# One-hot rows laid out by pairs of tokens, a reordered copy out of PSUM, and eleven low halves moved from DMA to VectorE, in a hybrid encoder layer

## The chip, the cores and the metric

The kernel runs on one core of one Trainium2 chip. The metric is the device time of one execution in microseconds (us). TensorE is PE in the profile (PEld is its weight load), VectorE is DVE, ScalarE is ACT, GpSimd is POOL, and SyncE, which issues most DMAs, is SP.

## What is computed

One encoder layer over 512 tokens of width 1024: a mixer (a gated linear recurrence beside chunked attention), cross-attention into 256 memory tokens, and an expert layer with 16384 single-neuron experts. Only the expert layer matters here. For each token, 8 heads select 16 experts each by product keys, so that a token has 128 selected experts with weights `g`:

```python
    def block(args):
        xt, it, gt = args
        u = expert_u[it]
        act = jax.nn.gelu(jnp.einsum('td,tkd->tk', xt, u))
        return jnp.einsum('tk,tkd->td', gt * act, expert_v[it])
```

An expert's number is `128 * i + j`, with `i` and `j` from the two key tables of its head.

## The kernel before

The first 128 tokens (tile 0) are done by gathering the rows of their experts. The other 384 tokens (tiles 1 to 3) are done densely: each of 128 blocks of 128 experts is multiplied with all 384 tokens, the result goes through the gelu and is multiplied by a dense weight that is zero where a token did not select the expert, and the second table then turns this into the output. Two things are therefore needed ahead of the dense second part, and the kernel makes them in the same stretch of its program.

**The dense weights.** For a token, the 128x128 matrix of weights is a product over its 128 selections: `hot` holds one-hot rows (column n of selection s is 1 where the expert's index equals n), `wei` holds the one-hot row of the other index times the weight, in two parts (a half-precision weight and its remainder). A group is four tokens. VectorE makes `hot` with one comparison (line 997) and `wei` with one product (line 1000), both 1024 half-precision elements per partition. PE then does eight matmuls (line 1003), two parts for each of four tokens, each with its own 128x128 weight load from `hot` and 128 columns of `wei`. ScalarE copies the result out of PSUM (line 1005) to a tile `stage`, which holds 16 tokens; when it is full, an SP DMA writes it to DRAM as `Wd` (line 1015, 1 MB). There are 96 groups and 24 such writes. The `hot` and `wei` tiles have three buffers each (`WGB`), `stage` has two. In the layout before, the token is the innermost index of `hot` and `wei`, with four tokens side by side: a matmul for one token reads every fourth element.

**The first multiplications, ahead.** Between the groups, PE multiplies expert blocks of the first table `U` with the 384 tokens (`mm1_parts`): 24 matmuls of 384 columns for each block, from a high half `wh` and a low half `wl` of the block (lines 111 to 113). ScalarE makes `wh` by a cast (line 131). The low half is `w - wh`, and it is made in one of two ways, which `source` decides by its third result: by DMA, where ScalarE writes `-w` rounded (line 137) and a POOL DMA then adds `w` to it (line 138); or by VectorE with one subtraction (line 149, in `fill_low`). `w`, `wh` and `wl` have three buffers each. Blocks 0 to 36 go by DMA, 37 and up by VectorE. Ten blocks are multiplied while VectorE prepares tile 1's selection; blocks 10 to 36 are spread over the 96 groups; then come blocks 37 to 39, and after these the second table's part, in which PE alternates between one block of `U` and one of `V`.

VectorE also does the selection of the next tile between the groups (`second_level`, lines 885 to 967). The order of instructions on each engine in this stretch comes from a scheduler that works at build time, from the program's order and priorities; from block 37 on the order is as written.

Of the kernel before, what the change touches and what calls it, by code (L numbers as in the profile page):

```python
# [12 lines left out]
F16 = mybir.dt.float16  # L13
# [3 lines left out]
AF = mybir.ActivationFunctionType  # L17
# [13 lines left out]
NE = 128  # L31
LAG = 40
# [4 lines left out]
NQ = 3  # L37
NORM_AT = (0, 6), (1, 2)
U_DMA = 3
U_V = ()  # L40
BY_DMA = ("pq",)
G_RATE = 2.45
G_END = 4
# [11 lines left out]
GS = float(2 ** 15)  # L55
# [20 lines left out]
def layer(ctx, tc, a, out, upto=99, dbg=None):  # L76
    nc = tc.nc
    dbg = dbg or {}
    V, A, PE, SP, PL = nc.vector, nc.scalar, nc.tensor, nc.sync, nc.gpsimd

    def pool(stack, name, bufs=1, **kw):
        return stack.enter_context(tc.tile_pool(name=name, bufs=bufs, **kw))
# [9 lines left out]
    def bank(name="bk"):  # L92
        return psum.tile([128, 512], F32, name=name, tag="bk")
# [65 lines left out]
    def source(kind, n):  # L159
# [5 lines left out]
        if kind == "U":  # L165
            return a["U"][n], [128, D], n < LAG - U_DMA and n not in U_V
        if kind == "V":
# [20 lines left out]
    def proj(key, ops, n=S, **kw):  # L188
        wh, wl = W.get(*key, **kw)
        ps = bank()  # L190
        mm3(ps[:, :n], [(wh[:, c], wl[:, c], h[:, :n], l[:, :n]) for c, (h, l) in enumerate(ops)])
        return ps
# [427 lines left out]
    for n in range(NCH):  # L620
        if n == 0:
            pair = close_pair(pair, [yo[c] for c in range(NCH)])
        ps = pair[n] if n < 2 else proj(("wo", n), [yo[c] for c in range(NCH)])
# [132 lines left out]
    with tc.tile_pool(name="hx", bufs=2) as hx:  # L756
        ho = []
        for c in range(NCH):
            t = hx.tile([128, S], F32, name="ht")
# [36 lines left out]
    def mm1_next():  # L796
        ahead[0] += 1
        return mm1_parts(ahead[0] - 1)

    top_pool = ExitStack()  # L800
    tp = pool(top_pool, "top")
    val = tp.tile([128, 8, 2, TT, 16], F32)
    idx = tp.tile([128, 8, 2, TT, 16], U32)

    io4 = tp.tile([128, NE, 4], F16)
    mio = tp.tile([128, 16, 8], F16)
    jr = tp.tile([128, 128], I32)
    PL.iota(jr, pattern=[[1, 128]], base=0, channel_multiplier=0)
    V.tensor_copy(io4, jr[:, :, None].to_broadcast([128, NE, 4]))
    V.tensor_copy(mio, jr[:, :16, None].to_broadcast([128, 16, 8]))  # L810


# [157 lines left out]
    def hurried(steps, offset):  # L970
        while True:
            with tc.high_priority(offset=offset) if offset else ExitStack():
                if next(steps, 0) == 0:
                    return
            yield

    with tc.tile_pool(name="wg", bufs=2) as wg, tc.tile_pool(name="st", bufs=2, side="right") as stages:
        parts, owed = iter(()), 0.0
        done = 0
        for k, _ in enumerate(hurried(second_level(1), OFF1)):  # L980
            while ahead[0] < LAG and done < (k + 1) * U_MID / 15 and done < U_MID:
                done += 1
                for _ in mm1_next():
                    pass
        rate = (LAG - SPARE - ahead[0]) * NCH / (DT * 32)
        for tile_ in range(1, TT):
            level = hurried(second_level((tile_ + 1) % TT), OFF2)
            ij, gg = SEL.pop(tile_)
            for q in range(8):
                tb = (tile_ - 1) * 8 + q  # L990
                stage = stages.tile([128, NE, 16], F32, name="stage", tag="stage")
                for t4 in range(0, 16, 4):
                    ps = bank()
                    gr = (q * 16 + t4) // 4
                    F4 = [128, 2, NE, 4]
                    hot = wg.tile(F4, F16, name="hot", bufs=WGB)
                    V.tensor_tensor(hot, io4[:, None].to_broadcast(F4), ij[:, gr, :, None].to_broadcast(F4),
                                    op=OP.is_equal)
                    wei = wg.tile(F4, F16, name="wei", bufs=WGB)
                    V.tensor_mul(wei, hot[:, 0:1].to_broadcast(F4), gg[:, gr, :, None].to_broadcast(F4))  # L1000
                    for k in range(4):
                        for part in range(2):
                            PE.matmul(ps[:, k * 128:(k + 1) * 128], hot[:, 1, :, k], wei[:, part, :, k],  # L1003
                                      start=part == 0, stop=part == 1)
                    A.activation(stage[:, :, t4:t4 + 4].rearrange("p i t -> p t i"),  # L1005
                                 ps.rearrange("p (t i) -> p t i", t=4), AF.Copy, scale=1.0 / GS)
                    if (q * 4 + t4 // 4) % LEVEL[1] < LEVEL[0]:
                        next(level, 0)
                    owed += rate
                    while owed >= 1:  # L1010
                        owed -= 1
                        if next(parts, 0) == 0 and ahead[0] < LAG - SPARE:
                            parts = mm1_next()
                            next(parts)
                SP.dma_start(Wd[:, tb], stage)
            for _ in level:
                pass
        for _ in parts:
            pass
        while ahead[0] < LAG - SPARE:  # L1020
            for _ in mm1_next():
                pass
        W.fill(W.used + 3)
# [227 lines left out]
```

## Time and profile before

| what | value |
| --- | --- |
| time, median of 3 runs | 1673.76 us (1672.78 to 1677.97) |
| the profiled execution's own time | 1675.25 us |
| its span, first to last instruction | 1673.5 us |
| busy share of the span: PE / DVE / ACT / POOL | 98% / 76% / 48% / 29% |
| first group of eight to the last, by the trace | about 549 to 757 us |
| mean granted TensorE clock | 0.996 |

Busy shares are means over a span whose stages have different limits. A busy PE is not a PE at its peak: a matmul's record lasts longer than the distance to the next matmul, so spacing is read from starts. A spacing times a count is PE's time; a mean length is not.

### The profile page before, as it was taken

How to read it: one execution, taken by the hardware profiler on the slowest of the kernel's cores; microseconds unless marked ns; L12 is line 12 of the kernel's file. 1: busy time of each engine (PE TensorE's matmuls, PEld its weight loads, DVE VectorE, ACT ScalarE, POOL GpSimd, SP SyncE). 2: the span in 40 equal slices, each digit the busy share in tenths (PEclk: the TensorE clock that was granted, in tenths of full speed). 3: DMA queues.
4: the chain of work that ended last, by engine and by line, in shares of the span. 5: the costliest groups of instructions: out<-in, count | busy, mean ns of one | idle time of the engine just before them, and what ended most of it. 6: DMA issues, size and time to landing. Idle time of an engine off the chain costs nothing.

```text
span 1673.5 us, 23775 instructions
## 1 busy us (share of the span) xinstructions
PE 1645.1 (98%) x8512; PEld 1443.6 (86%) x8512; DVE 1276.9 (76%) x2571; ACT 810.0 (48%) x1233; POOL 478.0 (29%) x346
## 2 busy tenths in 40 slices
PE   8999999999999999999999999999999999999997
PEld 6778888887779999999999999999999999988886
DVE  6778885555999888765777777777777777788887
ACT  5568753446446778873333333333333333333334
POOL 0010000001111111104544444445444445454331
PEclk9999999999999999999999999999999999999999
DMA  6345352127677898889988898898988988989994
GB/s 240 115 128 153 114 172 93 59 89 198 148 176 179 231 276 252 267 256 327 310 310 302 296 322 298 295 310 312 306 300 296 327 296 300 312 315 336 320 329 149
DMA packets 156934, 410.54 MB, mean 245 GB/s; under 512 B 13856, under 2 KB 62112, under 8 KB 153744
## 3 DMA queue, kind: packets, MB, share of 16 engines
q1 hardware_dynamic: 110016, 242.36, 42.5%
q0 software_dynamic: 46800, 166.68, 33.2%
q8 instruction: 66, 1.08, 0.3%
q14 instruction: 52, 0.43, 0.1%
HBM read 348.69 MB, written 29.36 MB: 226 GB/s over the span
## 4 chain that ended last, share of the span: by engine, by line
PE 88%; DVE 6%; DMA 2%; issue 2%; ACT 1%; SPq 0%; DVEq 0%; POOL 0%; POOLq 0%; ACTq 0%
PE acc L1106 31%; PE bk L111 15%; PE bk L113 15%; PE bk L112 15%; PE bk L1003 5%; DMA wl<-w 1%; PE pv L111 1%; PE pv L112 1%; PE pv L113 1%; DVE s L855 1%; DVE idx L853 1%; PE om L111 1%; PE om L112 1%; PE om L113 1%; DVE idx L859 1%
## 5 line engine op out<-in xcount | busy, mean ns | idle before, releaser
L131 ACT CAST wh<-w 128x1024 fp32r<-128x1024 f32 (+1 forms) x333 | 350.0, 1051 | 361.7 <-PE acc L1106 182.8
L111 PE MATMUL bk<-hH,wh 128*128 128x384 f32 (+1 forms) x1128 | 394.1, 349 | 0.0
L113 PE MATMUL bk<-hH,wl 128*128 128x384 f32 (+1 forms) x1128 | 386.1, 342 | 2.9 <-DMA wl<-w 2.7
L112 PE MATMUL bk<-hL,wh 128*128 128x384 f32 (+1 forms) x1128 | 385.3, 342 | 0.0
L149 DVE TENSOR_TENSOR wl<-w,wh 128x1024 fp32r<-128x1024 f32 (+1 forms) x280 | 340.2, 1215 | 27.8 <-ACT wh L131 27.1
L1036 POOL DMA_INDIRECT g<-in_Un,gidx x128 | 208.0, 1625 | 221.4 <-DVE junk L1043 210.7
L1036 POOL DMA_INDIRECT g<-in_V,gidx x128 | 202.1, 1579 | 240.0 <-DVE gacc L1053 225.1
L1106 PE MATMUL acc<-wh,ph 128*128 128x512 f32 x768 | 238.6, 391 | 0.0
L1106 PE MATMUL acc<-wh,pl 128*128 128x512 f32 x768 | 238.2, 391 | 0.0
L1106 PE MATMUL acc<-wl,ph 128*128 128x512 f32 x768 | 238.0, 390 | 0.0
L1083 DVE TENSOR_TENSOR pl<-act,ph 128x384 fp32r<-128x384 f32 x128 | 71.2, 557 | 199.9 <-ACT ph L1080 199.8
L111 PEld LDWEIGHTS bk<-hH,wh 128*128 128x128 f32 x1128 | 214.5, 190 | 7.3
L113 PEld LDWEIGHTS bk<-hH,wl 128*128 128x128 f32 x1128 | 212.4, 188 | 9.0 <-DMA wl<-w 4.7
L112 PEld LDWEIGHTS bk<-hL,wh 128*128 128x128 f32 x1128 | 213.3, 189 | 7.1
L787 ACT ACTIVATE act<-bk 128x384 f32<-128x384 f32 x128 | 63.6, 497 | 276.4 <-PE bk L113 276.4
L138 POOL DMA_DIRECT2D wl<-w x53 | 45.5, 858 | 522.7 <-ACT wl L137 431.3
L1106 PEld LDWEIGHTS acc<-wl,ph 128*128 128x128 f32 x768 | 144.1, 188 | 31.6
L1106 PEld LDWEIGHTS acc<-wh,pl 128*128 128x128 f32 x768 | 144.1, 188 | 31.1
L1106 PEld LDWEIGHTS acc<-wh,ph 128*128 128x128 f32 x768 | 142.9, 188 | 24.3
L1053 DVE SCALAR_TENSOR_TENSOR gacc<-g,gu,gacc 128x1024 f32<-128x1024 f32 x127 | 162.5, 1279 | 0.6
L1043 DVE SCALAR_TENSOR_TENSOR junk<-g,htok 128x1024 bf16<-128x1024 f32 x128 | 156.0, 1219 | 0.8
L1005 ACT ACTIVATE stage<-bk 128x512 f32<-128x512 f32 x96 | 102.9, 1097 | 39.9 <-PE bk L1003 34.9
(312 smaller groups left out, 2334.4 us busy)
## 6 DMA issues: line engine op xcount, KB each, us to landing
w<-in_U SPq DMA_DIRECT2D x128, 512.0 KB, 5.4
w<-in_V SPq DMA_DIRECT2D x128, 512.0 KB, 5.6
wl<-w POOLq DMA_DIRECT2D x53, 512.0 KB, 5.5
Wd<-stage SPq DMA_DIRECT2D x24, 1024.0 KB, 6.3
wt<-Wd SPq DMA_DIRECT2D x90, 256.0 KB, 7.0
w<-in_w_pq SPq DMA_DIRECT2D x16, 512.0 KB, 3.7
w<-in_w_in SPq DMA_DIRECT2D x15, 512.0 KB, 3.8
x<-in_xT SPq DMA_DIRECT2D x16, 256.0 KB, 6.0
```

The costliest lines, as they stand in the source:

```text
L111: PE.matmul(ps, lh, rh, start=first and c == 0, stop=False)
L112: PE.matmul(ps, lh, rl, start=False, stop=False)
L113: PE.matmul(ps, ll, rh, start=False, stop=last and c == n - 1)
L131: A.copy(wh[:, cs], w[:, cs])
L149: V.tensor_sub(wl[:, cs], w[:, cs], wh[:, cs].bitcast(F32))
L1003: PE.matmul(ps[:, k * 128:(k + 1) * 128], hot[:, 1, :, k], wei[:, part, :, k], start=part == 0, stop=part == 1)
L1005: A.activation(stage[:, :, t4:t4 + 4].rearrange("p i t -> p t i"), ps.rearrange("p (t i) -> p t i", t=4), AF.Copy, scale=1.0 / GS)
L1036: PL.indirect_dma_start(out=g, out_offset=None, in_=a[table], in_offset=bass.IndirectOffsetOnAxis(ap=gidx[:, k:k + 1], axis=0))
L1043: V.scalar_tensor_tensor(junk, g, 1.0, htok, op0=OP.mult, op1=OP.mult, accum_out=gu[:, st:st + 1])
L1053: V.scalar_tensor_tensor(gacc, g, gu[:, k:k + 1], gacc, op0=OP.mult, op1=OP.add)
L1083: V.tensor_sub(PS[e][1], ACT.pop(e), PS[e][0].bitcast(F32))
L1106: PE.matmul(acc[t, hf], lhs[:, ts], rhs[:, hf * 512:(hf + 1) * 512], start=e == 0 and part == 0, stop=e == NE - 1 and part == 2)
```

## The change

Three edits. **Pairs:** `hot` and `wei` are laid out by pairs of tokens, with two tokens innermost in place of four, so a matmul for one token reads every second element of a contiguous piece; the comparison and the product run over the same 1024 elements, with the selected index and the weight now repeated in runs of two. **The copy:** ScalarE's copy walks in the order of `stage` (expert index outside, four tokens inside): it writes runs of four neighbouring elements to `stage` and reads PSUM with a step of 128 elements from one to the next; before, it read PSUM straight through and wrote every sixteenth element. **Low halves:** `U_V` names blocks 26 to 39, so that blocks 26 to 36, eleven of them, get their low half from VectorE in place of ScalarE and a POOL DMA (37 to 39 had it from VectorE before).

```diff
-U_V = ()
+U_V = range(26, LAG)
...
-    io4 = tp.tile([128, NE, 4], F16)
+    io2 = tp.tile([128, NE, 2], F16)
...
-                    F4 = [128, 2, NE, 4]
+
+                    pairs = lambda x: x[:, gr].rearrange("p s (q k) -> p (s q) k", k=2)
+                    F4 = [128, 4, NE, 2]
                     hot = wg.tile(F4, F16, name="hot", bufs=WGB)
-                    V.tensor_tensor(hot, io4[:, None].to_broadcast(F4), ij[:, gr, :, None].to_broadcast(F4),
+                    V.tensor_tensor(hot, io2[:, None].to_broadcast(F4), pairs(ij)[:, :, None].to_broadcast(F4),
                                     op=OP.is_equal)
                     wei = wg.tile(F4, F16, name="wei", bufs=WGB)
-                    V.tensor_mul(wei, hot[:, 0:1].to_broadcast(F4), gg[:, gr, :, None].to_broadcast(F4))
+                    W4 = [128, 2, 2, NE, 2]
+                    V.tensor_mul(wei.rearrange("p (s q) n k -> p s q n k", s=2),
+                                 hot[:, None, 0:2].to_broadcast(W4),
+                                 gg[:, gr].rearrange("p s (q k) -> p s q k", k=2)[:, :, :, None].to_broadcast(W4))
                     for k in range(4):
                         for part in range(2):
-                            PE.matmul(ps[:, k * 128:(k + 1) * 128], hot[:, 1, :, k], wei[:, part, :, k],
-                                      start=part == 0, stop=part == 1)
-                    A.activation(stage[:, :, t4:t4 + 4].rearrange("p i t -> p t i"),
-                                 ps.rearrange("p (t i) -> p t i", t=4), AF.Copy, scale=1.0 / GS)
+                            PE.matmul(ps[:, k * 128:(k + 1) * 128], hot[:, 2 + k // 2, :, k % 2],
+                                      wei[:, 2 * part + k // 2, :, k % 2], start=part == 0, stop=part == 1)
+                    A.activation(stage[:, :, t4:t4 + 4], ps.rearrange("p (t i) -> p i t", t=4), AF.Copy,
+                                 scale=1.0 / GS)
```

VectorE's queue in the second half of the stretch, from the last step of the selection's weights on (`hot` and `wei` are the groups' tiles, `eq`, `rc`, `kn` and `sel` belong to the selection, `wl` is a block's low half; the numbers are the builder's names of buffers). Before:

```order
L967 SCALAR_TENSOR_TENSOR gg_7054<-bk_7049,gg_7054 128x32x4
L997 TENSOR_TENSOR hot_7141<-io4_3894,ij_6183 128x1024
L936 TENSOR_TENSOR eq_7653<-eq_7653 128x1024
L1000 TENSOR_TENSOR wei_7143<-hot_7141,gg_6184 128x1024
L997 TENSOR_TENSOR hot_7161<-io4_3894,ij_6183 128x1024
L936 TENSOR_TENSOR eq_7653<-eq_7653 128x512
L1000 TENSOR_TENSOR wei_7163<-hot_7161,gg_6184 128x1024
L997 TENSOR_TENSOR hot_7186<-io4_3894,ij_6183 128x1024
```

The same place now (lines 997 and 1000 have become 999 and 1003):

```order
L967 SCALAR_TENSOR_TENSOR gg_7050<-bk_7045,gg_7050 128x32x4
L999 TENSOR_TENSOR hot_7109<-io2_3894,ij_6183 128x1024
L999 TENSOR_TENSOR hot_7136<-io2_3894,ij_6183 128x1024
L1003 TENSOR_TENSOR wei_7111<-hot_7109,gg_6184 128x1024
L1003 TENSOR_TENSOR wei_7138<-hot_7136,gg_6184 128x1024
L931 TENSOR_TENSOR eq_7643<-rc_7578,mio_3895 128x2048
L999 TENSOR_TENSOR hot_7156<-io2_3894,ij_6183 128x1024
L933 TENSOR_TENSOR eq_7643<-eq_7643,kn_7641 128x2048
L1003 TENSOR_TENSOR wei_7158<-hot_7156,gg_6184 128x1024
L999 TENSOR_TENSOR hot_7181<-io2_3894,ij_6183 128x1024
L149 TENSOR_TENSOR wl_7203<-w_7122,wh_7123 128x1024
L1003 TENSOR_TENSOR wei_7183<-hot_7181,gg_6184 128x1024
```

A subtraction (`L149`) now stands in the queue between a group's `hot` and its `wei`, about every three to four groups, eleven times; the selection's steps stand a few groups later. Each subtraction stands three to five groups ahead of its block's first matmul on PE, and behind the cast of its `wh`.

ScalarE's queue in the same half of the stretch (`act` is a block's gelu). Before:

```order
L1005 ACTIVATE stage_7089<-bk_7090 128x4x128
L131 CAST wh_7127<-w_7126 128x1024
L787 ACTIVATE act_7110<-bk_7031 128x384
L1005 ACTIVATE stage_7089<-bk_7112 128x4x128
L137 ACTIVATE wl_7130<-w_7126 128x1024
L1005 ACTIVATE stage_7089<-bk_7140 128x4x128
L1005 ACTIVATE stage_7089<-bk_7160 128x4x128
L1005 ACTIVATE stage_7184<-bk_7185 128x4x128
L131 CAST wh_7205<-w_7204 128x1024
```

And now (line 1005 has become 1010):

```order
L1010 ACTIVATE stage_7085<-bk_7135 128x128x4
L1010 ACTIVATE stage_7085<-bk_7155 128x128x4
L1010 ACTIVATE stage_7179<-bk_7180 128x128x4
L131 CAST wh_7200<-w_7199 128x1024
L787 ACTIVATE act_7197<-bk_7128 128x384
L1010 ACTIVATE stage_7179<-bk_7209 128x128x4
L1010 ACTIVATE stage_7179<-bk_7229 128x128x4
L1010 ACTIVATE stage_7179<-bk_7249 128x128x4
L131 CAST wh_7295<-w_7294 128x1024
```

The eleven `wl` steps of line 137 are gone from ScalarE's queue, and so are the eleven DMAs of line 138 behind them on POOL's (53 before, 42 now). The copy has the same 512 elements per partition in another order. PE's queue has the same instructions; one or two of a block's matmuls stand on the other side of a group here and there.

## Rows read from the trace of the kernel before

**Rows 1.** The page, parts 1 and 4: engines, and the last chain by line.

```profile
PE 1645.1 (98%) x8512; PEld 1443.6 (86%) x8512; DVE 1276.9 (76%) x2571; ACT 810.0 (48%) x1233; POOL 478.0 (29%) x346
...
PE acc L1106 31%; PE bk L111 15%; PE bk L113 15%; PE bk L112 15%; PE bk L1003 5%; DMA wl<-w 1%; PE pv L111 1%; PE pv L112 1%; PE pv L113 1%; DVE s L855 1%; DVE idx L853 1%; PE om L111 1%; PE om L112 1%; PE om L113 1%; DVE idx L859 1%
```

**Rows 2.** Windows: busy time per engine (instructions), granted clock, DMA share.

```profile
core 0: us, PE busy (x) PEld busy (x) DVE busy (x) ACT busy (x) POOL busy (x), PEclk, DMA share, GB/s
...
530.00:540.00 10.00, 7.97 (x44) 7.51 (x44) 10.00 (x76) 5.72 (x8) 1.44 (x3) 1.00 0.99 245
...
549.00:657.00 108.00, 107.80 (x740) 98.74 (x739) 93.93 (x266) 86.11 (x101) 12.28 (x15) 1.00 0.87 252
657.00:757.00 100.00, 100.00 (x688) 91.93 (x687) 71.56 (x118) 78.56 (x91) 9.43 (x11) 1.00 0.88 265
...
757.00:800.00 43.00, 43.00 (x231) 40.55 (x230) 26.63 (x38) 16.02 (x24) 21.11 (x14) 1.00 0.95 334
800.00:1600.00 800.00, 800.00 (x3981) 719.94 (x3979) 608.82 (x767) 281.26 (x388) 378.42 (x234) 1.00 0.90 309
```

**Rows 3.** Chain that ended last, 549 to 757 us: by line, one piece.

```profile
by line: PE bk L1003 43.5%; PE bk L111 18.4%; PE bk L113 18.4%; PE bk L112 18.2%; DMA wl<-w 3.0%; PE bk L959 0.3%; issue 0.0%
...
645.27 0.96 PE bk L1003 x8
```

**Rows 4.** Timeline of PE around a group of eight: start, length, instruction.

```profile
644.93 0.34 PE L113 MATMUL bk<-hH,wl 128*128 128x384 f32 x1
645.11 1.12 PE L1003 MATMUL bk<-wei,hot 128*128 128x128 f16 x8
645.98 0.43 PE L111 MATMUL bk<-hH,wh 128*128 128x384 f32 x1
646.25 0.34 PE L112 MATMUL bk<-hL,wh 128*128 128x384 f32 x1
```

**Rows 5.** PE matmuls by form, whole span: busy us, mean ns, idle before.

```profile
L1003 PE MATMUL bk<-wei,hot 128*128 128x128 f16 x768 | 107.4, 296 | 0.0
...
L522 PE MATMUL po<-ph,v 128*128 128x384 f32 x8 | 2.7, 337 | 0.0
...
L522 PE MATMUL po<-ph,v 128*128 128x256 f32 x8 | 2.2, 281 | 0.0
...
L522 PE MATMUL po<-ph,v 128*128 128x128 f32 x8 | 1.8, 223 | 0.0
```

**Rows 6.** VectorE groups by form, whole span.

```profile
L149 DVE TENSOR_TENSOR wl<-w,wh 128x1024 fp32r<-128x1024 f32 x278 | 338.8, 1219 | 25.8 <-ACT wh L131 25.0 <-PE bk L1003 0.6
...
L997 DVE TENSOR_TENSOR hot<-io,ij 128x1024 f16<-128x1024 f16 x96 | 66.2, 691 | 36.8 <-PE bk L1003 35.6
L1000 DVE TENSOR_TENSOR wei<-hot,gg 128x1024 f16<-128x1024 f16 x96 | 65.4, 686 | 0.8
```

**Rows 7.** ScalarE groups by form, whole span.

```profile
L1005 ACT ACTIVATE stage<-bk 128x512 f32<-128x512 f32 x96 | 102.9, 1097 | 39.9 <-PE bk L1003 34.9 <-DMA Wd<-stage 1.7 <-ACT kn L929 1.4
...
L137 ACT ACTIVATE wl<-w 128x1024 fp32r<-128x1024 f32 x53 | 56.8, 1071 | 0.0
...
L101 ACT CAST qh<-bk 128x512 fp32r<-128x512 f32 x13 | 7.5, 579 | 0.0
...
L929 ACT CAST kn<-idx 128x128 f16<-128x128 uint32 x8 | 6.4, 796 | 0.5 <-DVE eq L933 0.5
...
L101 ACT CAST k<-kr 128x128 fp32r<-128x128 f32 x16 | 4.8, 306 | 1.5 <-DMA kr<-in_keysT 1.5
```

**Rows 8.** DMA, 549 to 657 us: queues, issues of low halves.

```profile
q1 hardware_dynamic: 3680, 19.14, 48.3%
q0 software_dynamic: 2170, 7.91, 38.6%
...
wl<-w POOLq DMA_DIRECT2D x15, 512.0 KB, 5.6
```

More of the change, by code (lines that the diff above doesn't have):

```diff
@@ L808, in layer @@
     PL.iota(jr, pattern=[[1, 128]], base=0, channel_multiplier=0)
-    V.tensor_copy(io4, jr[:, :, None].to_broadcast([128, NE, 4]))
+    V.tensor_copy(io2, jr[:, :, None].to_broadcast([128, NE, 2]))
     V.tensor_copy(mio, jr[:, :16, None].to_broadcast([128, 16, 8]))
```

## The prediction, made before the changed kernel was run

> **What bounds the kernel now.** I read the page first: PE is busy 98% of the span, and the chain that ended last names the eight-matmul groups of line 1003 with 5% [rows 1]. A mean over stages says little about this change, so I then cut the trace into windows. Groups run from 549 to 757 us. There the reader is to see that PE is busy without a gap, that VectorE has 93.9 of 108 us and then 71.6 of 100, ScalarE 86.1 and 78.6, and that the DMA engines are busy 0.87 and 0.88 of the time [rows 2]. PE is the bound, and three others stand close behind it. The chain inside that stretch agrees: 43.5% of it is line 1003, 55% the 384-column matmuls of `U`, one wait for a low half's DMA stands at its start, and there is no VectorE or ScalarE in it [rows 3]. After the stretch PE is busy all of the time up to 1600 us [rows 2]: whatever the stretch gets shorter by, everything behind it moves forward by the same, because it is a fixed amount of PE work.
>
> What a group costs on PE is read from starts. The chain has 0.96 us for eight matmuls [rows 3], and the timeline gives the same: from 645.11 to 646.25 us are the eight and one L111 matmul, whose usual distance to the next is 0.18 (644.93 to 645.11), so the eight have 0.96 us, 120 ns each [rows 4]. Of the 208 us, 96 x 0.96 = 92 are the groups and 116 the `U` blocks.
>
> **Pairs, on PE.** Is 120 ns for 128 columns much? Line 522 has matmuls of 128, 256 and 384 columns that lie side by side: 223, 281 and 337 ns, so 128 columns cost 57 ns. The 128 columns of line 1003, of which neighbours lie four elements (8 bytes) apart, have 296 ns: 73 more than the 223 [rows 5]. That is what reading at about half the rate would give. The pairs put neighbours 4 bytes apart, which is also the distance of neighbours in line 522's 4-byte data, at the full rate. No row shows half-precision data read at that step, so the saving for a matmul lies between 0 and 73 ns. I take 49 (120 becomes about 71): nearer to line 522, as its bytes lie at the new distance, but under 57, since the weight load before each matmul must now hide behind less. That is 8 x 49 = 0.39 us a group, and 37 us of PE time over 96 groups, far more than will be gained, because the others stop it first.
>
> **Pairs, on VectorE.** `hot` and `wei` take 691 and 686 ns for 1024 elements, while the subtraction of 1024 4-byte elements takes 1219 [rows 6]: half-precision runs of four go two at a time. No row has runs of two. Bounds: 691 and 686 as now, or up to 1219 each. I take no change, since a run of two still holds one whole pair. The smaller `io2` conversion, once, costs less than before and lies ahead of the groups.
>
> **The copy.** 512 elements out of PSUM in 1097 ns; the same count read and written straight takes 579 [rows 7]: the scattered write costs some 520 ns. Afterwards the write goes in runs of four and the read jumps. No row has a jumping read of PSUM. Bounds: 579, and upwards the dearest scattered access that ScalarE shows, 128 elements in 796 ns against 306 straight, 3.8 ns an element [rows 7], which would make 579 + 512 x 3.8 = 2.5 us. I take 0.6 to 1.1. Within that it costs nothing and gives nothing: ScalarE's other work is 86.1 - 50 x 1.10 = 31 us in the first window's 50 groups and 28 in the second's 46, so that with 1.1 us copies it stays at 86 and 79. Its cover ends near 1.3 us in the first window (31 + 50 x 1.3 = 96).
>
> **Low halves.** Eleven steps of 1071 ns leave ScalarE [rows 7] and eleven DMAs leave POOL's queue, which nothing behind them waits for before the stretch ends. On the DMA engines one such low half is dear: 38.6% of 108 us over 15 of them is 2.8 us each [rows 8]; eleven make 31 us, all of it for blocks 26 to 36, which is about the second window. VectorE gets 11 x 1219 ns = 13.4 us [rows 6], in the second window alone. The subtraction waits for the cast of `wh`; behind it in VectorE's queue stand the group's `wei` and all later groups, for which PE waits. Over its 278 present uses that wait is 25.0 us, 0.09 each [rows 6]; at worst each of the eleven waits for one whole cast, 11 x 1.07 = 12 us. I take 3, since it stands three to five groups ahead of its block and PE has up to two groups ready.
>
> **The sum.** First window (108 us): PE 107.8 - 50 x 0.39 = 88; VectorE 94; DMA 0.87 x 108 = 94. VectorE and DMA tie, and each can be filled: from 530 to 540 us VectorE was busy 10.00 of 10.00 and the DMA engines 0.99 [rows 2]. Together they will not reach this; I take 98, a gain of 10. Second window (100 us): PE 100 - 46 x 0.39 = 82; VectorE 71.6 + 13.4 = 85; DMA 88 - 31 = 57; ScalarE 67 or less. The bound is VectorE; with 3 us of waits, and one for its steps standing unevenly, 89, a gain of 11. Together 21 us: the span of 1673.5 becomes 1652.5, and the profiled execution's 1675.25 becomes 1654. The three runs' median is 1.5 us lower than that execution, less than what counts here; I predict 1654. This hardly depends on the 49 ns: any spacing under about 90 ns leaves PE below 96 and 89. A measurement of this kernel can tell about 0.3%, 5 us, from no change.
>
> **A. The step is not what the eight matmuls cost.** Then the spacing stays at 120 ns, for the weight load or the half-precision operand itself might set it. Against it is the 73 ns over line 522; for it, that those rows differ in data type as well. PE stays the bound in both windows, VectorE's 85 of 100 fits beneath it, and the DMA relief lies under it: 1674, 1671 to 1677. Chance 0.14. [...]
>
> **B. The reordered read of PSUM is dear** (ends slower). ScalarE needs 31 + 28 - 12 = 47 us besides the copies; with 96 copies of x us it fills the present 208 us at x = 1.67, and from there each further 0.1 us costs 10 us. At the upper bound of 2.5 us: 47 + 240 = 287, 79 more than 208: 1753; at 2.0 us: 1705. For it: scattered accesses are what is dear in every such row. Against: the dearest price is that of 2-byte writes, and the present scattered access of this same copy costs 1.0 ns an element, which as a read makes 1.1 us. Chance 0.09. [...]
>
> **C. VectorE loses its two at a time** (slower). Both products go to about 1219 ns, 1.06 us more a group: 94 + 53 = 147 and 85 + 49 = 134 us, 281 in place of 208: 1747. It decides from where the two together take (208 - 179) / 96 = 0.3 us more a group. Against it: runs of four already go at double rate with one operand that repeats. Chance 0.06.
>
> **D. The subtractions hold up VectorE's queue.** With the full 12 us of waits the second window is VectorE's 97, and the gain is the first window's 10 and 3 more: 1661. If the DMA engines give no more than 0.9 in the first window, as in the 800 us up to 1600 [rows 2], that window is 104 and the gain 4 + 11: 1659. Either is faster still; chance 0.12.
>
> **How the numbers follow.** The forecast, a gain of 15 to 29 us with 1654 as its likeliest, has 0.59; D 0.12, A 0.14, B 0.09, C 0.06. Faster: 0.59 + 0.12 = 0.71; within 0.3%: A, 0.14; slower: 0.15. The lowest time that the other engines allow is VectorE's alone, 94 + 85 = 179 of 208 us, 1646 with the own time's offset; four more for rows that a faster copy or quieter DMA engines shorten: 1642. Upwards the range takes in D and A: 1677. What it leaves out, B, C and a little below, is under 0.2.
>
> **What would show it.** Right: the L1003 matmuls near 223 ns in place of 296 and about 0.57 us for eight in the chain; idle time of PE before L1003's weight loads that waits for `wei` or `hot`, and no more idle time of `hot` that waits for PE; VectorE above 0.95 in both windows; `hot` and `wei` still near 690; the copy under 1.3 us; DMA share near 0.95 before block 26 and 0.65 after. The group stretch is then some 187 us long. Wrong: 296 ns again (A); a copy above 1.6 us with ScalarE busy throughout (B); `hot` over 0.8 us (C); VectorE idle before line 149 by over half a us each (D). It would also be wrong if the PE work behind the stretch started no earlier, because the last of `Wd` or of the `U` blocks came no earlier.

## The result, and the profile after

The changed kernel takes 1644.15 us (median of four runs, 1643.66 to 1645.27), the kernel before 1673.86 us beside it (1672.78 to 1677.97): a ratio of 0.9819 (95% interval 0.9802 to 0.9836), 30 us less. The profiled execution took 1643.93 us, its span is 1642.1 us. The forecast was 1654 with 1642 to 1677 as its range: right in direction and mechanism, with the gain put 10 us too small.

The page, parts 1 and 4, which answer to [rows 1]:

```profile
PE 1609.1 (98%) x8512; PEld 1407.3 (86%) x8512; DVE 1280.6 (78%) x2582; ACT 757.0 (46%) x1222; POOL 467.3 (28%) x335
...
PE acc L1111 31%; PE bk L111 15%; PE bk L113 15%; PE bk L112 15%; DMA wl<-w 2%; PE bk L1008 2%; PE pv L111 1%; PE pv L112 1%; PE pv L113 1%; DVE s L855 1%; DVE idx L853 1%; PE om L111 1%; PE om L112 1%; PE om L113 1%; DVE idx L859 1%
```

PE is busy 36 us less, with as many instructions, and the groups' line (1008, it was 1003) has fallen from 5% of the chain to 2%.

The 96 groups now start at 552.7 and end at 723.9 us, 171 us in place of 206. The windows of the first 50 groups, the other 46, and what lies behind them, as in [rows 2]:

```profile
core 0: us, PE busy (x) PEld busy (x) DVE busy (x) ACT busy (x) POOL busy (x), PEclk, DMA share, GB/s
552.70:643.50 90.80, 87.34 (x740) 77.77 (x739) 89.19 (x263) 63.11 (x99) 12.00 (x14) 1.00 0.99 290
643.50:723.90 80.40, 79.08 (x676) 70.81 (x675) 78.00 (x129) 47.99 (x80) 0.00 (x0) 1.00 0.72 257
724.00:800.00 76.00, 76.00 (x399) 70.80 (x398) 51.40 (x73) 27.03 (x38) 35.66 (x24) 1.00 0.93 323
800.00:1570.00 770.00, 770.00 (x3827) 692.49 (x3827) 586.08 (x734) 270.60 (x374) 363.33 (x226) 1.00 0.90 309
```

PE is no longer full in the first two windows. In the first, VectorE is busy 89.2 of 90.8 us and the DMA engines 0.99 of the time, both at once; in the second, VectorE 78.0 of 80.4, while the DMA engines have come down to 0.72. Behind the groups PE is full as before, so the gain is carried to the end: the last group comes 31.7 us earlier (755.6 to 723.9), the end of the span 31.4.

A group on PE, against [rows 4]:

```profile
564.14 0.34 PE L113 MATMUL bk<-hH,wl 128*128 128x384 f32 x1
564.32 0.64 PE L1008 MATMUL bk<-wei,hot 128*128 128x128 f16 x8
564.76 0.42 PE L111 MATMUL bk<-hH,wh 128*128 128x384 f32 x1
565.02 0.34 PE L112 MATMUL bk<-hL,wh 128*128 128x384 f32 x1
```

From 564.32 to 565.02 us are eight matmuls and one of L111; less the L111's usual 0.18 that leaves 0.52 us, and the chain below has 0.48, where it was 0.96. From one start to the next within a group are 58 ns (median over all 768; before 118 by the same reading).

The same operations as in [rows 5 to 7], by form:

```profile
L1008 PE MATMUL bk<-wei,hot 128*128 128x128 f16 x768 | 61.9, 221 | 2.8 <-DVE wei L1003 1.5 <-ACT stage L1010 1.0
...
L999 DVE TENSOR_TENSOR hot<-io,ij 128x1024 f16<-128x1024 f16 x96 | 64.3, 680 | 0.3 <-PE bk L1008 0.2
L1003 DVE TENSOR_TENSOR wei<-hot,gg 128x1024 f16<-128x1024 f16 x96 | 64.7, 684 | 0.0
...
L1010 ACT ACTIVATE stage<-bk 128x512 f32<-128x512 f32 x96 | 56.6, 610 | 56.5 <-PE bk L1008 29.2 <-DMA Wd<-stage 21.3 <-PE bk L112 3.5
```

The matmul went from 296 to 221 ns, `hot` and `wei` hardly moved (680 and 684), the copy went from 1097 to 610. `hot` used to wait 35.6 us for PE [rows 6]; now 0.2. A wait that has grown is the copy's, from 1.7 us [rows 7] to 21.3, for the write of `Wd` out of one of the two `stage` tiles.

The chain from 549 to 735 us, by line, and its pieces from 589.9 on (start, length, what):

```profile
by line: PE bk L111 17.4%; PE bk L1008 16.7%; PE bk L113 16.3%; PE bk L112 15.8%; DMA wl<-w 11.0%; issue 9.4%; DMA Wd<-stage 3.3%; DVE hot L999 2.9%; DVE wei L1003 2.7%; DVE wl L149 1.9%; DVE eq L931 0.6%; ACT wh L131 0.5%; ACT stage L1010 
...
589.91 6.15 issue
...
596.27 6.05 issue
602.34 10.16 DMA wl<-w
...
627.64 10.28 DMA wl<-w
...
638.36 6.12 DMA Wd<-stage
...
646.65 1.23 DVE wl L149
647.87 0.60 DVE wei L1003
648.47 0.60 DVE hot L999
...
715.49 0.48 PE bk L1008 x8
```

The reader is to see three stages: PE alone up to 590 us, then accumulating DMAs and a `Wd` write up to 645 (with PE between them from 612 to 624), then VectorE up to 665, and PE again after that. The two pieces of `issue` are time for which the view names no cause; both end where GpSimd's queue issues a low half's DMA (596.1 and 602.3 us). In [rows 3] there was PE nearly from end to end.

### The profile page after: what moved, and what is told of

Same layout as the page of the kernel before. It is cut to its first block, busy times and chain, and to the rows that moved or that the text cites. A ratio compares the mean times of both kernels' runs of the same rounds, so it can differ in the third digit from the quotient of the medians.

```text
span 1642.1 us, 23756 instructions
## 1 busy us (share of the span) xinstructions
PE 1609.1 (98%) x8512; PEld 1407.3 (86%) x8512; DVE 1280.6 (78%) x2582; ACT 757.0 (46%) x1222; POOL 467.3 (28%) x335
## 4 chain that ended last, share of the span: by engine, by line
PE 86%; DVE 7%; DMA 3%; issue 2%; ACT 1%; SPq 0%; DVEq 0%; POOL 0%; POOLq 0%; ACTq 0%
PE acc L1111 31%; PE bk L111 15%; PE bk L113 15%; PE bk L112 15%; DMA wl<-w 2%; PE bk L1008 2%; PE pv L111 1%; PE pv L112 1%; PE pv L113 1%; DVE s L855 1%; DVE idx L853 1%; PE om L111 1%; PE om L112 1%; PE om L113 1%; DVE idx L859 1%
## 5 line engine op out<-in xcount | busy, mean ns | idle before, releaser
L111 PE MATMUL bk<-hH,wh 128*128 128x384 f32 (+1 forms) x1128 | 394.2, 349 | 0.0
L149 DVE TENSOR_TENSOR wl<-w,wh 128x1024 fp32r<-128x1024 f32 (+1 forms) x291 | 353.7, 1216 | 27.9 <-ACT wh L131 27.6
L111 PEld LDWEIGHTS bk<-hH,wh 128*128 128x128 f32 x1128 | 213.5, 189 | 7.3
L138 POOL DMA_DIRECT2D wl<-w x42 | 36.1, 859 | 433.8 <-ACT wl L137 339.5
L111 PE MATMUL bk<-oh,wh 128*128 128x512 f32 x280 | 113.0, 405 | 2.4 <-ACT oh L105 2.4
```

The source lines that it names most:

```text
L111: PE.matmul(ps, lh, rh, start=first and c == 0, stop=False)
L138: PL.dma_start(wl, w, accum_op=OP.add)
L149: V.tensor_sub(wl[:, cs], w[:, cs], wh[:, cs].bitcast(F32))
```

## The experiments

Theory 1: the step at which PE reads half-precision operands doubles what the eight matmuls cost, and that is the gain; once it is gone, the DMA engines and VectorE share the bound. Theory 2: the gain comes from the load that the copy and the low halves take off ScalarE and the DMA engines. Each run was timed beside the kernel before.

| run | us, median | ratio to before, 95% interval | groups, first to last, us |
| --- | --- | --- | --- |
| change | 1644.15 | 0.9802 to 0.9836 | 171 |
| e1 pairs alone | 1655.40 | 0.9874 to 0.9904 | 179 |
| e2 copy and low halves, no pairs | 1674.85 | 0.9988 to 1.0008 | 205 |
| e3 pairs and low halves, old copy | 1645.28 | 0.9815 to 0.9842 | 174 |
| e4 pairs and copy, low halves as before | 1649.06 | 0.9835 to 0.9862 | 180 |
| e5 token outermost | 1742.26 | 1.0383 to 1.0420 | 272 |
| e6 weights by fours, moving by pairs | 1655.31 (one) | | 180 |
| e7 weights by pairs, moving by fours | 1675.27 (one) | | 204 |
| e8 low halves, every second block from 16 | 1647.12 | 0.9802 to 0.9844 | 175 |
| e9 low halves by GpSimd, 10 to 36 | 1684.11 | 1.0032 to 1.0058 | 210 |
| e10 low halves by GpSimd, 10 to 25 | 1670.72 | 0.9952 to 0.9977 | 197 |
| e11 low halves by VectorE from 31 | 1641.98 | 0.9784 to 0.9810 | 173 |
| e12 no adding DMA for 10 to 25 | 1638.59 | 0.9761 to 0.9789 | 168 |

The last column is read from the profiled execution, whose own time can lie some us off the median: 1651 for e1, 1653 for e4, 1641 for e12.

### One part at a time: e1 to e4

e1, the change with the old copy and the old way to the low halves:

```diff
-U_V = range(26, LAG)
+U_V = ()
...
-                    A.activation(stage[:, :, t4:t4 + 4], ps.rearrange("p (t i) -> p i t", t=4), AF.Copy,
-                                 scale=1.0 / GS)
+                    A.activation(stage[:, :, t4:t4 + 4].rearrange("p i t -> p t i"),
+                                 ps.rearrange("p (t i) -> p t i", t=4), AF.Copy, scale=1.0 / GS)
```

> Pairs alone: the old copy and the low halves of blocks 26 to 36 by DMA, as before. Theory 1 (the step at which PE reads is what the eight matmuls cost): the matmul takes 218 ns and the eight 0.48 us, as after the change; PE needs some 162 us of the stretch, but the DMA engines still carry 0.87 to 0.88 of 206 us, 181 us of work, so they set the end: a stretch of 185 to 190 us, 1656 to 1662 us. Theory 2 (the gain comes from the load that the copy and the low halves take off ScalarE and the DMA engines): under 5 us gained, 1669 to 1676.

e2 is the kernel before with those two edits the other way round (`U_V = range(26, LAG)` and the new copy).

> The reordered copy and the low halves by VectorE, with the old layout by fours. Theory 1: PE still needs 96 x 0.96 + 116 = 208 us, the copy takes 0.6 us and the DMA share falls in the second half, and the time stays: 1671 to 1677 us. Theory 2: most of the gain is there without the pairs: 1650 to 1660.

e3 is the change with only the copy put back, e4 the change with only `U_V = ()`.

> Pairs and low halves by VectorE, with the old copy (1.1 us). Theory 1: ScalarE had room: in the first window it goes from 69 to about 69 + 48 x 0.5 = 93 of 101 us, still under the DMA engines and VectorE, so 1644 to 1649 us. Theory 2 (the copy carries part of the gain): ScalarE at 93 of 101 us is late for the casts and for stage, 1650 to 1658.

> Pairs and the reordered copy, with the low halves of blocks 26 to 36 by DMA as before. Theory 1 as to PE, with the DMA engines as the next bound: their 181 us of work stay, the share is 0.97 or more through the whole stretch, which is 183 to 190 us long: 1656 to 1660 us, the same as the pairs alone. Rival (the low halves are hidden anyway, and moving them gave nothing): 1643 to 1647. Theory 2: 1665 to 1676.

The pairs alone bring about 20 us, and without them the other two edits bring nothing: 0.9998, in a kernel whose copy takes 597 ns and whose DMA engines are busy 0.73 of the groups' time. Theory 2 falls. With the pairs and the new copy in place the low halves are worth 5 us (e4 to the change: 1649 to 1644; the two intervals just meet at 0.9835, and no execution of e4 is as fast as any of the change), which lies between the two expectations of e4: not hidden, and less than a bound by the DMA engines alone would give. Beside the old copy they are worth 10 us (e1 to e3: 1655 to 1645). The copy is worth nothing that can be told when the low halves are with VectorE (e3 and the change overlap), and 6 us when they are not (e1 to e4, whose intervals do not touch). e1 was a little faster than expected; its windows of the first 50 and the other 46 groups show why it stops there:

```profile
551.00:642.10 91.10, 87.17 (x741) 77.99 (x739) 89.32 (x265) 81.88 (x99) 12.01 (x14) 1.00 0.97 288
642.10:730.10 88.00, 80.73 (x676) 72.03 (x675) 69.17 (x117) 74.46 (x90) 9.43 (x11) 0.98 0.96 295
```

The DMA share is 0.97 and 0.96, 173 us of work. In the second part VectorE has 19 us of room, and PE still waits. What the low halves buy is the second part's 88 that becomes 80.4; the first part is as long as in the change.

One more thing shows in e4's profiled execution, which with 1653 us is the slowest of its five:

```profile
700.00:735.00 35.00, 31.05 (x239) 27.61 (x238) 20.55 (x29) 17.22 (x28) 2.57 (x3) 0.90 0.94 307
```

The granted clock was 0.97 from 650 to 700 us, where PE was busy 47.97 of 50.00 us, and 0.90 here, where it was busy 31.05 of 35.00; in the change it is 1.00 in both. What lowered it is not shown. That is no part of the 5 us, since e4's median execution (1649.06) has a mean clock of 0.996, above the change's 0.991 to 0.994.

### Which read it is: e5 to e7

e6 splits the comparison in two and lays out by fours the half of `hot` that PE loads as weights; e7 does so with `wei` and the half of `hot` that it is made from.

```diff
+                    hj = hot[:, 2:4].rearrange("p q n k -> p (q n k)").rearrange("p (n k) -> p n k", k=4)
+                    V.tensor_tensor(hj, io4, ij[:, gr, 1, None].to_broadcast(Q4), op=OP.is_equal)
...
-                            PE.matmul(ps[:, k * 128:(k + 1) * 128], hot[:, 2 + k // 2, :, k % 2],
+                            PE.matmul(ps[:, k * 128:(k + 1) * 128], hj[:, :, k],
```

> The changed kernel, but the half of hot that PE loads as weights is laid out by fours (8 bytes apart), wei by pairs (4 bytes); hot is then made by two comparisons of 512 elements. Theory a (the moving operand's read sets the spacing): spacing 58 to 70 ns, matmul 218 ns, weight load 117 ns; time 1644 to 1655 us with the second comparison's start-up on VectorE. Theory b (the weight load sets it): spacing near 117 ns, the eight at 0.95 us; 1665 to 1680.

> The reverse: the weights by pairs, wei (which PE streams) by fours. Theory a: spacing near 118 ns, matmul near 297 ns, weight load 97 ns; 1665 to 1680 us. Theory b: spacing 58 to 70 ns; 1644 to 1655. If each of the two alone leaves 118 ns, both reads set it and the change needed both.

The matmul and its weight load by form, of e6 and then of e7:

```profile
L1012 PE MATMUL bk<-wei,hot 128*128 128x128 f16 x768 | 65.5, 227 | 6.1 <-DVE wei L1007 5.9
...
L1012 PEld LDWEIGHTS <-hot 128*128 128x128 f16 x768 | 49.7, 117 | 22.4 <-DVE wei L1007 10.9 <-issue 4.5 <-DVE hot L1004 3.1
```

```profile
L1010 PE MATMUL bk<-wei,hot 128*128 128x128 f16 x768 | 105.3, 294 | 0.0
...
L1010 PEld LDWEIGHTS <-hot 128*128 128x128 f16 x768 | 77.6, 112 | 15.4 <-DVE hot L1003 8.3 <-DVE wei L1007 2.8 <-issue 2.1
```

With the weights by fours the matmul has 227 ns and its spacing is 60 ns; with the moving operand by fours it is 294 and 117, and the time is that of the kernel before. The weight load is longer at 8 bytes too (in e6 117 against the change's 98), but with a spacing of 60 ns it does not set the spacing. So it is the streamed operand, theory a. One expectation was missed: e7's load, whose weights lie by pairs, was to take 97 ns and takes 112. Its first load in a group has a median of 97 there; from the third on, behind e7's slow matmuls, they have 115 to 118. So a long load record has two causes here, and 117 ns alone does not tell which; e6, with fast matmuls, is the run that shows the stride's part. e6 pays 11 us for something else: two comparisons of 512 take 422 and 418 ns where one of 1024 took 680, 15 us more of VectorE over 96 groups. That VectorE has no room for them (it is busy 179.4 of 186 us from 549 to 735 in e6) is the same tie seen from another side.

e5 puts the token outermost, so that PE reads 2-byte neighbours and VectorE's repeated value changes only every 128 elements:

```diff
...
-                    pairs = lambda x: x[:, gr].rearrange("p s (q k) -> p (s q) k", k=2)
-                    F4 = [128, 4, NE, 2]
+                    F4 = [128, 8, NE]
                     hot = wg.tile(F4, F16, name="hot", bufs=WGB)
-                    V.tensor_tensor(hot, io2[:, None].to_broadcast(F4), pairs(ij)[:, :, None].to_broadcast(F4),
-                                    op=OP.is_equal)
+                    V.tensor_tensor(hot, io1[:, None].to_broadcast(F4),
+                                    ij[:, gr].rearrange("p s k -> p (s k)")[:, :, None].to_broadcast(F4), op=OP.is_equal)
...
```

> The changed kernel with the token outermost in hot and wei: a matmul reads neighbours 2 bytes apart. If PE is at full rate from 4 bytes downwards, the spacing of the eight stays at 58 ns; if it still gains, it goes under 55. The other side is VectorE's price for runs of one: if it still goes two at a time, hot and wei stay near 680 ns and the time is 1640 to 1648 us; if it loses that (as the 1219 ns of a 1024-element subtraction), they take about 1.2 us each, VectorE needs some 96 x 2 x 0.54 = 104 us more in the stretch, and the time is 1720 to 1755 us.

```profile
L1002 DVE TENSOR_TENSOR wei<-hot,gg 128x1024 f16<-128x1024 f16 x96 | 115.5, 1221 | 0.0
L998 DVE TENSOR_TENSOR hot<-io,ij 128x1024 f16<-128x1024 f16 x96 | 114.3, 1216 | 0.0
```

By form, `hot` and `wei` go from 680 to 1216 and 1221 ns, and the kernel is 4% slower than before, though PE's spacing is 56 ns: from 4 bytes down to 2 PE gains next to nothing. Of the three layouts only runs of two have both engines near their best: PE's spacing is 58 ns, against 118 with runs of four and 56 with runs of one, and `hot` takes 680 ns, against 691 [rows 6] and 1216. What in the runs of one costs VectorE its rate, no run shows.

### What holds the groups now: e8 to e12

e8 and e11 only change which blocks VectorE takes: `(*range(16, 37, 2), 37, 38, 39)` and `range(31, LAG)`.

> The changed kernel, but the eleven low halves that VectorE takes are every second one of blocks 16 to 36 in place of 26 to 36: the same counts, spread. Theory c (from 590 to 645 us the DMA engines, share 1.00, are what PE waits for, while they have room later): five low halves of 2.8 us leave that stretch, VectorE gets 6 us there and loses 6 later: the stretch falls from 171 towards PE's own 162 us, 1635 to 1641 us. Theory d (VectorE, 97% busy there, is as much the bound): 1643 to 1649.

> The changed kernel, but VectorE takes the low halves from block 31 on; 26 to 30 go by DMA as before the change. VectorE loses 6 us just where the chain has it (646 to 665 us), the DMA engines get 14 us. If the DMA engines are the closer bound, this is between the changed kernel (1644) and the one without the low halves (1649): 1645 to 1649. If VectorE is, under 1644.

The first 50 groups of e8, and its chain in these and in the other 46:

```profile
552.30:643.00 90.70, 86.36 (x735) 77.15 (x735) 85.15 (x200) 58.03 (x93) 7.71 (x9) 1.00 0.88 268
by line: DMA Wd<-stage 20.5%; DMA wl<-w 15.1%; PE bk L1008 10.3%; DMA w<-in_U 9.6%; PE bk L111 9.4%; PE bk L113 8.5%; PE bk L112 8.4%; issue 4.2%; DVE wei L1003 3.6%; DVE hot L999 3.2%; ACT wh L131 3.0%; DVE wl L149 2.5%; ACT stage L1010 1.
by line: DVE wei L1003 26.0%; DVE hot L999 24.9%; DMA Wd<-stage 10.4%; DVE wl L149 5.7%; issue 4.2%; DVE eq L936 2.7%; DVE eq L933 2.7%; DVE eq L931 2.7%; PE bk L1008 2.3%; DVE pos L898 2.1%; DVE pos L906 2.1%; DVE c L901 2.0%; DVE tops L89
```

e8 refutes theory c: with a DMA share of 0.88 its first 50 groups take as long as the change's (90.7 us, VectorE busy 85.2). It does not show theory d there: in that part transfers have 45% of the chain and `wei` and `hot` 7%, while neither the DMA engines nor VectorE are full, so what held it stays open. `wei` and `hot` have 51% in the second part. e11 has six subtractions of blocks 31 to 36 in place of eleven. Its 1642 us lie on VectorE's side of the expectation, but the interval overlaps that of the change, so the two are not told apart: five low halves moved from VectorE back to the DMA engines change nothing that can be measured. Two bounds that stand side by side look like that.

e9 and e10 let GpSimd subtract (the edit of e9; e10 has `range(10, 26)` in `U_P`):

```diff
-U_V = range(26, LAG)
+U_V = range(10, LAG)
+U_P = range(10, 37)
...
-                        V.tensor_sub(wl[:, cs], w[:, cs], wh[:, cs].bitcast(F32))
+                        sub = PL if key[0] == "U" and key[1] in U_P else V
+                        sub.tensor_sub(wl[:, cs], w[:, cs], wh[:, cs].bitcast(F32))
```

> The changed kernel, but the low halves of blocks 10 to 36 are subtractions by GpSimd, in place of 16 accumulating DMAs and 11 subtractions by VectorE. GpSimd's product of 128x512 takes 1.28 us, so by an estimate 2.6 us for 1024, 69 us over the stretch, in an engine that is 13% busy. The DMA engines lose 16 x 2.8 = 45 us and VectorE 13 us. Theory e (after the change the stretch of 171 us was held by the DMA engines and VectorE together): PE alone is left, 96 x 0.48 + 116 = 162 us, so 1634 to 1639 us. Rival f (GpSimd's work slows VectorE, or is late for its block): VectorE's 680 ns go up or PE waits for wl, 1644 to 1665.

> As the run before, but only blocks 10 to 25 by GpSimd; 26 to 36 stay with VectorE as in the changed kernel. This takes away the DMA load alone (share 1.00 from 549 to 650 us), and leaves VectorE's. If the DMA engines held that part, PE is free of waits up to 645 us and the rest stays: 1637 to 1641 us. If VectorE did: 1643 to 1646. With rival f: later.

Both are far slower, e9 even slower than the kernel before, and both lie beyond the 1665 us that e9's expectation gave rival f; the mechanism is rival f's, in both its halves. The timeline of e9 shows the first half, first VectorE and then GpSimd (start, length, instruction, idle before):

```profile
586.75 0.67 DVE L1005 TENSOR_TENSOR wei<-hot,gg 128x1024 f16<-128x1024 f16 x1
...
587.57 2.74 DVE L1001 TENSOR_TENSOR hot<-io,ij 128x1024 f16<-128x1024 f16 x1
...
590.45 0.67 DVE L1005 TENSOR_TENSOR wei<-hot,gg 128x1024 f16<-128x1024 f16 x1
```

```profile
587.38 2.38 POOL L151 TENSOR_TENSOR wl<-w,wh 128x1024 fp32r<-128x1024 f32 x1 [6.10 <-ACT wh L132]
```

GpSimd subtracts from 587.38 to 589.76; the `hot` that VectorE starts in that time ends at 590.31, 0.55 us after GpSimd, which is about what it needs alone. Beside 20 of e9's 27 subtractions a `hot` or `wei` is held in this way and ends 0.55 us after the subtraction, which reads as standing still and not as running slowly. The second half is GpSimd's being late, in its timeline and in the chain:

```profile
614.64 19.69 POOL L151 TENSOR_TENSOR wl<-w,wh 128x1024 fp32r<-128x1024 f32 x2 [6.85 <-ACT wh L132]
...
620.43 11.59 POOL wl L151
...
704.64 9.58 POOL wl L151
```

The first of the two subtractions from 614.64 us on takes 17.4 us (up to 632.02, by the chain), while VectorE runs 26 instructions beside it, each at its usual length; another, at 699.29, takes 14.9, where most take 2.4 to 3.0. So in e9 each of the two engines is held up beside the other, VectorE's `hot` by some 2 us and GpSimd, in these two cases, by 12 to 15, and PE's matmuls wait 7.8 us for these low halves. These two runs do not answer what they were made for, the DMA load of the first part.

e12 does. It leaves the adding DMA out for blocks 10 to 25, so that the result lacks their low halves:

```diff
-                    PL.dma_start(wl, w, accum_op=OP.add)
+                    if key[0] != "U" or key[1] not in range(10, 26):
+                        PL.dma_start(wl, w, accum_op=OP.add)
```

> The changed kernel without the accumulating DMAs of blocks 10 to 25: ScalarE still writes the rounded -w, but w is not added, so the low half of these blocks is left out of the result. This takes 16 x 2.8 = 45 us of DMA work out of the stretch and touches neither VectorE nor GpSimd's arithmetic. If the DMA engines alone held the part from 590 to 645 us, PE has no waits there, the stretch is 163 to 166 us and the time 1635 to 1639 us. If VectorE, 97% busy there, holds it just as well, the stretch stays at 169 to 172 us: 1641 to 1645, with the chain on hot, wei and the selection in that part.

Its windows for the first 50 and the other 46 groups, and its chain from 549 to 735 us by line:

```profile
553.10:640.00 86.90, 86.42 (x741) 77.98 (x739) 86.90 (x257) 65.20 (x101) 0.00 (x0) 1.00 0.61 224
640.00:720.90 80.90, 78.99 (x677) 70.86 (x675) 79.78 (x135) 47.62 (x78) 0.00 (x0) 1.00 0.66 235
```

```profile
by line: DVE hot L1000 20.3%; DVE wei L1004 18.9%; PE bk L111 10.6%; PE bk L112 9.7%; PE bk L113 9.7%; PE bk L1009 9.2%; DVE pos L907 1.9%; DVE wl L150 1.9%; DVE eq L934 1.9%; DVE pos L899 1.9%; DVE eq L937 1.8%; DVE c L902 1.8%; DVE eq L93
```

The time is within the first expectation (1639), the stretch of 168 us between the two, and the chain has become VectorE's, as the second said. Some 37 us of DMA work less in the first part (0.99 of 90.8 us, then 0.61 of 86.9) shorten it by only 4 us, from 90.8 to 86.9, and there VectorE is busy 86.90 of 86.90. So the low halves' DMAs are the bound of the first part, 4 us ahead of VectorE; in the second nothing changes (80.9 against 80.4), as it has no such DMAs either way. Whether it is the load of the DMA engines or the time that one low half takes to land (10.2 and 10.3 us in the change's chain, a median of 5.6 before [rows 8]) is not told apart, since e12 takes away both; with a share of 0.99 the load is the plainer reading, while e8's first part, as long at a share of 0.88, would fit the landing.

## Why the prediction was right, and by how much it was off

**What bounds the kernel.** PE's groups did; e2 shows that neither the copy nor the low halves were worth removing first.

**Pairs, on PE.** The mechanism was right, the term too small: 49 ns of the 120 was taken, 60 came (118 to 58), 0.48 us a group in place of 0.39. The rate is that of line 522, 57 to 58 ns for 128 columns [rows 5]; the discount for a weight load that "must now hide behind less" was not needed, since e6, with a load of 117 ns, has a spacing of 60. As the prediction said, the time hardly depends on it. That the step of the streamed operand sets the spacing is what e7 and e6 show, with 117 ns at 8 bytes and 60 at 4.

**Pairs, on VectorE.** No change was taken, 680 and 684 came. That a run of two "still holds one whole pair" was an assumption; the runs show the times of `hot` for runs of four, two and one (691, 680, 1216 ns), not their cause. Rival C needed runs of one: e5 has its price, 1.22 us each, and its time, 1742 for the 1747 worked out.

**The copy.** It came out at the lower bound: 610 ns, against 579 for a straight one. Reading PSUM with a jump cost ScalarE nothing much (31 ns); writing with a jump had cost 490 (1097 less 610). Rival B falls. That the copy gives nothing holds beside the moved low halves (e3); e1 and e4 show 6 us without them.

**Low halves.** The second part's DMA share fell from 0.88 to 0.72. Between the first and the last group the subtractions waited 1.4 us for a cast, once, where 3 us was taken and 12 was rival D's bound:

```profile
L149 DVE TENSOR_TENSOR wl<-w,wh 128x1024 fp32r<-128x1024 f32 x13 | 15.8, 1212 | 1.4 <-ACT wh L131 1.4
```

(Two longer waits, of 3.8 and 3.5 us, lie behind the last group; the kernel before has the same two there, with 5.3 and 3.5.) The pieces of the chain from 646.65 us on show VectorE holding PE for some 18 us behind that one wait. The low halves are worth 5 us (e4).

**The sum** is the step that failed in size: 98 and 89 us for the two parts, 187 together (1.4 of it behind the last group), against 90.8 and 80.4. Two things were wrong in it. First, "Together they will not reach this": VectorE and the DMA engines did, 98% and 0.99 at the same time. Second, VectorE's 94 and 85 were sums of busy time, and a wait inflates that. Two subtractions and products of the change side by side, VectorE's timeline:

```profile
672.12 1.22 DVE L149 TENSOR_TENSOR wl<-w,wh 128x1024 fp32r<-128x1024 f32 x1
673.26 0.68 DVE L1003 TENSOR_TENSOR wei<-hot,gg 128x1024 f16<-128x1024 f16 x1
673.86 0.68 DVE L999 TENSOR_TENSOR hot<-io,ij 128x1024 f16<-128x1024 f16 x1
```

A record of 0.68 us is followed after 0.60, one of 1.22 after 1.14. So an instruction that is followed by a wait adds 0.08 us more to the busy time than one that is followed at once, and before the change `hot` waited for PE 61 times up to 735 us alone: about 5 us. The same work, with eleven subtractions more, came to 89.2 + 78.0 = 167 us in place of 179. A tally of both traces gives most of the twelve: between the first and the last group VectorE's work is broken by idle time 106 times before the change and 5 times after it, 8 us at 0.08 each; the eleven subtractions, back to back, add 1 us less than their records; `hot`, 691 ns before and 680 now, gives 1; and 0.7 lay outside the groups. The prediction had this rule for PE, spacing and not length, and did not use it on VectorE. By the same error its lowest time that the other engines allow, 1646, came out 2 us above what was measured; only the four further us of the range took that in. And of the 14 us by which the two parts together were put too long, the groups' start, 3 us later than before, hid 3.

What is left above PE's own need, worked out from its spacing (0.48 in place of 0.96 us for each group: 108 - 50 x 0.48 = 84 and 98 - 46 x 0.48 = 76 us), is 7 us in the first part and 4 in the second. The groups also started 3 us later than before, which is why 35 us off the stretch are 31 to 32 at its end; the versions e1 to e12 started anywhere from 548.9 to 556.4, and I have not found why.

**Behind the groups** the gain was carried on one to one, as forecast. Rivals A (e7 has its spacing and its time), B and C did not come. Of D, one wait of 1.4 us came for its 12, and the DMA engines gave 0.99 of the first part and not 0.9.

## What to carry to other kernels

When a matmul costs twice the spacing of another with as many columns, look at the distance between neighbours of its moving operand, and choose the layout in which PE and the engine that writes it both keep their rate: here runs of two half-precision elements (58 ns from matmul to matmul, 680 ns for `hot`), while four cost PE half its rate (117 ns, e7) and one cost VectorE nearly half of its (1216 ns, e5). Where three engines stand within 15% of each other, price a gain by the next bound, and count that engine's work by start-to-start spacing, since busy time that contains many waits is too long (here 179 us were reckoned from it and 167 came). An edit that is worth nothing ahead of the bound (the low halves, with the copy, in e2) can be worth 5 us once the bound has moved, so it is tried again after each such step.

## What the runs showed that I had not expected

In e9 a GpSimd subtraction (`wl` from `w` and `wh`) held up the `hot` or `wei` that VectorE started beside it: 2.74 us for a `hot` of 0.67, ending 0.55 us after GpSimd's instruction. GpSimd's was held up in its turn, 17.4 us for one beside 26 instructions of VectorE, where most take 2.4 to 3.0. `hot` takes a mean of 0.94 us there in place of 0.68 over the window from 549 to 735 us, and the two together turned 58 us of relief (by estimate 45 us of DMA, 13 of VectorE) into 40 us lost.

In these runs, with half-precision elements, the stride of the streamed operand halved PE's rate at 8 bytes (117 ns from matmul to matmul, e7) and not at 4 (58, the change); the stride of the weights lengthened their load from 98 ns (the change) to 117, with the spacing still 60 ns (e6).
